# Local attention by halves of head pairs, with row factors in the exponential and rotary rows gathered by DMA

## The chip, the cores and the metric

The kernel runs on one core of a Trainium2 chip. The metric is device time in microseconds for one execution. Each core has TensorE (PE, matrix products, whose weight loads are shown apart as PEld), VectorE (DVE), ScalarE (ACT), GpSimd (POOL) and a queue engine (SP) that here issues nearly all DMA transfers. Each engine works through its own instructions in the order in which they were built; an instruction that waits holds up all behind it on its engine.

## The reference

A decoder of two layers, model width 1024, 512 tokens and 16 meta tokens ahead of them. Layer 0 mixes tokens by gated linear attention, layer 1 by sliding-window attention over one shared set of keys and values. Around each mixer stand two feed-forward blocks. Every block has a norm before it and one after. The part that matters here is the mixer of layer 1 (cut):

```python
q = (hn @ w_q)                          # hn = rmsnorm(h): 16 heads of 64, 4 query heads per key head
q = apply_partial_rope(q, cos, sin) * 64 ** -0.5       # the first 16 of 64 columns are rotated
# per block of 128 queries: 16 meta keys, 128 keys of the block before, 128 of its own
s = jnp.einsum('bkgnqd,bknsd->bkgnqs', q_blk, k_band)
mask: meta all visible; previous block j > i and blk > 0; own block j <= i
m = jnp.maximum(jnp.max(s, axis=-1, keepdims=True), sink)
p = jnp.exp(s - m)
p = p / (jnp.sum(p, axis=-1, keepdims=True) + jnp.exp(sink - m))
o = p @ v_band ; mix = o @ w_out
```

The norm's factor is one number for each token (row factor): the projection can use the unnormed rows, and the factor can be applied to q later.

## The kernel before

Activations lie transposed: 128 channels on the partitions, tokens along the row. A float32 operand is split into a high and a low part (`split`, L405; `split_part`, L224), and a product takes three matmuls (`mm3s`, L333). Weights come as 128x512 raw tiles, in eight buffers, by DMAs that SP issues (`load_unit`, L274). ACT copies the high part and DVE subtracts it for the low part.

What sets the order: every stage is written as generator jobs under `Flow` (L60), a clock of estimates that only matmuls advance. A job says by `yield` how long its results will take, and the recorded instructions of a job are put between the matmuls of the main thread. The framework then fixes the order on each engine when it builds the program. PSUM has eight tiles (`pp`, L133).

Layer 1's mixer is `swa` (L1062). `x_first` (L509) does the projection of the first four of eight units for tokens in two groups of 256, while the residual step of the block before (`Residual.run`, L453) still makes the operands of the second group, on DVE and ACT. `x_units` (L486) does units 4 to 7, 512 tokens wide. One unit is a pair of heads, which share the 128 partitions (e = 0 and 1). `evac` (L1079) takes each result out of PSUM with `rope` (L997), four DVE operations over all 128 channels. The row factor of each token, spread over all partitions by a matmul (`rstd`, L348, tile r_l1m) and copied by ACT, is first multiplied into the tables of cosine and sine (tile csq, L1083), so q leaves `rope` with factor, rotation and 1/8 in it.

`soft` (L1095) is the first half of attention for one unit. It makes scores for four blocks and two heads (tile sc), copies them to SBUF (L1118) and masks by copy_predicated (L1119, tile s, or Y for the first units). Then follow the maximum (L1123), the exponential with the sum (L1131, tile den), and the division: the meta part goes to tile mt (L1139), head 0 by DVE (L1144), head 1 by ACT (L1142). `core` (L1146) transposes the probabilities (L1160, tile pt, and ptm for the meta part), copies them (L1165), masks a second copy (L1166) and multiplies by the values (tile o, L1176 to L1181). Own and previous block are one product with the previous block's values and one with the difference (dv). `split` makes so, the operand of `out_proj` (L552), which gives y: units 0 to 3 first, 512 tokens wide, written to Y; then units 4 to 7, 256 wide and added. A unit waits for the second unit before it, and units 4 to 7 for the core of the third before it (`LAG`, L48).

## Time and profile before

| | us |
|---|---|
| median of 3 runs (1934.33 to 1935.24) | 1934.42 |
| the profiled execution | 1935.17 |
| its span | 1933.4 |
| PE busy in the span | 1888.9 |
| first scores of the mixer start at | 1431.7 |
| 256-wide half of its output projection starts at | 1538.1 |

The times of a trace are counted from the start of the span. A row of a window lists start and end, its length, the busy time of PE, PEld, DVE, ACT and POOL with the number of instructions, the granted clock (1.00 is full), the share of the DMA engines and GB/s. A row of a wait names who waited for whom, the total in us, how many times, and the longest. A row of the chain has a start, a length, and what ran then. A group has busy time, mean ns of one, and idle time before it with what ended it. Where two operations follow each other on one engine they overlap by some 0.1 us, so a chain's length by its count is less than the duration of one.

### The profile page before, as it was taken

How to read it: one execution, taken by the hardware profiler on the slowest of the kernel's cores; microseconds unless marked ns; L12 is line 12 of the kernel's file. 1: busy time of each engine (PE TensorE's matmuls, PEld its weight loads, DVE VectorE, ACT ScalarE, POOL GpSimd, SP SyncE). 2: the span in 40 equal slices, each digit the busy share in tenths (PEclk: the TensorE clock that was granted, in tenths of full speed). 3: DMA queues.
4: the chain of work that ended last, by engine and by line, in shares of the span. 5: the costliest groups of instructions: out<-in, count | busy, mean ns of one | idle time of the engine just before them, and what ended most of it. 6: DMA issues, size and time to landing. Idle time of an engine off the chain costs nothing.

```text
span 1933.4 us, 37344 instructions
## 1 busy us (share of the span) xinstructions
PE 1888.9 (98%) x14522; PEld 1802.5 (93%) x14522; DVE 1408.0 (73%) x2853; ACT 1017.9 (53%) x2308; POOL 176.3 (9%) x377
## 2 busy tenths in 40 slices
PE   8999999999999999999999999999998999999997
PEld 8999999999999999999999898989976898989897
DVE  6885858676364788585887786868787679858584
ACT  5663636653245555353574453535647865636363
POOL 2000000321111300000032000000310040000002
PEclk9999999999999999999999999999998999999998
DMA  4332323322113123333351123233321112333331
GB/s 161 107 98 89 105 91 110 110 77 72 39 56 110 56 72 98 100 92 104 98 173 45 61 88 115 89 109 101 130 66 34 63 49 82 96 103 109 102 111 44
DMA packets 102145, 174.55 MB, mean 90 GB/s; under 512 B 11472, under 2 KB 24272, under 8 KB 101968
## 3 DMA queue, kind: packets, MB, share of 16 engines
q1 hardware_dynamic: 101680, 172.05, 28.3%
q8 instruction: 113, 1.85, 0.4%
q14 instruction: 64, 0.52, 0.1%
q10 hardware_dynamic: 288, 0.13, 0.0%
HBM read 170.04 MB, written 2.10 MB: 89 GB/s over the span
## 4 chain that ended last, share of the span: by engine, by line
PE 69%; DVE 19%; ACT 8%; issue 3%; POOL 1%; DMA 0%; SPq 0%; DVEq 0%; ACTq 0%; POOLq 0%
PE y L162 30%; PE x L162 17%; PE a L162 10%; DVE raw L251 5%; DVE w_s L246 4%; PE c L162 3%; ACT w_s L245 3%; DVE w L246 3%; PE d L162 2%; PE o L162 1%; DVE w L227 1%; PE po L162 1%; ACT w L226 1%; DVE hidl1f L775 1%; PE sc L162 1%
## 5 line engine op out<-in xcount | busy, mean ns | idle before, releaser
L246 DVE TENSOR_TENSOR w_s<-raw,w_s 128x512 fp32r<-128x512 f32 x288 | 194.1, 691 | 134.9 <-ACT w_s L245 133.1
L227 DVE TENSOR_TENSOR w<-raw,w 128x512 fp32r<-128x512 f32 x378 | 239.4, 658 | 33.4 <-ACT w L226 31.6
L162 PE MATMUL y<-hidl0f,w 128*128 128x256 f32 (+1 forms) x2112 | 261.1, 285 | 0.0
L162 PEld LDWEIGHTS y<-hidl0f,w 128*128 128x128 f32 x2112 | 258.8, 188 | 0.7
L245 ACT ACTIVATE w_s<-raw 128x512 fp32r<-128x512 f32 x288 | 175.3, 628 | 152.6 <-DVE raw L251 139.3
L162 PE MATMUL y<-hidl1f,w 128*128 128x512 f32 (+1 forms) x1344 | 249.6, 346 | 0.0
L162 PEld LDWEIGHTS y<-hidl1f,w 128*128 128x128 f32 x1344 | 212.3, 188 | 34.1 <-ACT hidl1f L774 0.5
L226 ACT ACTIVATE w<-raw 128x512 fp32r<-128x512 f32 x378 | 209.2, 587 | 49.7 <-PE y L162 42.3
L251 DVE TENSOR_TENSOR raw<-raw,raw 128x512 f32<-128x512 f32 x288 | 198.1, 688 | 5.5
L403 POOL TENSOR_TENSOR acc_post<-acc_post,sq_post 128x256 f32<-128x256 f32 (+1 forms) x72 | 56.9, 791 | 1493.8 <-ACT sq_post L402 1493.0
L246 DVE TENSOR_TENSOR w<-raw,w 128x512 fp32r<-128x512 f32 x216 | 148.3, 688 | 31.1 <-ACT w L245 29.7
L162 PE MATMUL x<-x_l0m,w 128*128 128x272 f32 (+1 forms) x1200 | 158.3, 288 | 0.0
L245 ACT ACTIVATE w<-raw 128x512 fp32r<-128x512 f32 x216 | 133.9, 621 | 41.2 <-PE y L162 40.9
L162 PEld LDWEIGHTS x<-x_l0m,w 128*128 128x128 f32 x1200 | 149.4, 189 | 1.2
L572 DVE TENSOR_TENSOR Y<-y,Y 128x256 f32<-128x256 f32 (+2 forms) x176 | 83.0, 473 | 73.0 <-PE y L162 72.7
L162 PE MATMUL a<-zl0f_t,w_s 128*128 128x264 f32 x864 | 117.8, 285 | 3.8 <-ACT c L751 3.8
L162 PE MATMUL a<-zl1f_t,w_s 128*128 128x256 f32 x864 | 115.0, 282 | 2.0 <-ACT c L751 1.5
L162 PEld LDWEIGHTS a<-zl0f_t,w_s 128*128 128x128 f32 x864 | 110.1, 188 | 5.0 <-ACT c L751 5.0
L162 PEld LDWEIGHTS a<-zl1f_t,w_s 128*128 128x128 f32 x864 | 106.8, 188 | 4.7 <-ACT c L751 4.6
L162 PE MATMUL x<-x_l0f,w 128*128 128x256 f32 (+1 forms) x768 | 101.7, 293 | 6.9 <-ACT w L226 5.9
L162 PEld LDWEIGHTS x<-x_l0f,w 128*128 128x128 f32 x768 | 98.3, 194 | 8.2 <-ACT w L226 6.1
L162 PE MATMUL x<-x_l1f,w 128*128 128x256 f32 (+1 forms) x576 | 93.1, 320 | 0.0
(488 smaller groups left out, 3281.9 us busy)
## 6 DMA issues: line engine op xcount, KB each, us to landing
raw<-in_w_in SPq DMA_DIRECT2D x352, 256.0 KB, 2.9
raw<-in_w_out SPq DMA_DIRECT2D x96, 256.0 KB, 3.4
raw<-in_gla_in SPq DMA_DIRECT2D x50, 256.0 KB, 3.0
raw<-in_w_last SPq DMA_DIRECT2D x48, 256.0 KB, 3.1
raw<-in_w_out SPq DMA_DIRECT2D x64, 128.0 KB, 2.9
raw<-in_gla_out SPq DMA_DIRECT2D x16, 256.0 KB, 2.8
raw<-in_w_q SPq DMA_DIRECT2D x16, 256.0 KB, 3.9
raw<-in_swa_out SPq DMA_DIRECT2D x16, 256.0 KB, 3.0
```

The lines of the kernel that those rows point to most:

```text
L162: inst = pe.matmul(o, lhs, rhs, start=start, stop=stop, skip_group_check=onto)
L226: act.activation(w[:, 0, :m], raw[:, :m], AF.Copy)
L227: dve.tensor_tensor(w[:, 1, :m], raw[:, :m], w[:, 0, :m].bitcast(F32), op=ALU.subtract)
L245: act.activation(w[:, 0, :512], src, AF.Copy)
L246: dve.tensor_tensor(w[:, 1, :512], src, w[:, 0, :512].bitcast(F32), op=ALU.subtract)
L251: dve.tensor_tensor(dst, dst, src, op=ALU.add)
L403: pool.tensor_tensor(sums[0][:, :n], sums[0][:, :n], t[:, :n], op=ALU.add)
L572: dve.tensor_tensor(y, p[:, :n], y, op=ALU.add)
L775: dve.scalar_tensor_tensor(t.hid[:, 1, g], t.h, -1.0, t.hid[:, 0, g].bitcast(F32), op0=ALU.mult, op1=ALU.subtract)
```

## The change

Attention runs in sixteen visits, each for one unit and one half of the tokens (two blocks): the first half of units 0 to 3, their second half, then the same for units 4 to 7. A visit's four score columns, 576 wide, are divided by one DVE multiply, and the meta part is copied afterwards.

The row factors are no longer spread over the partitions. `root` (the first part of the old `rstd`) leaves them as columns, tokens on the partitions (tile roots). They enter as the scale of the exponential, and are multiplied into the maximum. So `evac` is one ACT copy with the factor 1/8 and waits for no factor, and neither does its drain in `x_first` and `x_units`.

The rotary rows, 16 of each head's 64, are gathered by eight DMAs of SP from the q tiles of four units into one tile of 128 partitions (`turn`), turned by four DVE operations, and put back by eight DMAs. There is a turn for each of the two token groups of units 0 to 3, and one for units 4 to 7. The tables in memory are laid out for it (cosp, sinp). The meta values need 64 partitions instead of 128. The second call of `out_proj` waits for the second halves of units 4 to 7 only ahead of its second token group. The diff, cut (in the body of `swa` mainly the added lines are shown; the lines that they replace stand in the listing above):

```diff
--- before.py
+++ after.py
@@ -45,7 +45,9 @@
 STAGGER = 5.0
 SOFT = 5.0
 NORM = 3.0
-LAG = 3
+LAG = 4
+TURN = 3.5
+PROBS = 1.4
 NEG = -1e30
 
 V_GAIN = 0
@@ -345,7 +347,7 @@
         mm3s([(o, w)], j, x, g, start, stop)
 
 
-    def rstd(sq, n, dim, half, name, eng=pool):
+    def root(sq, n, dim, name, eng, yv=None):
         c = 128 if n % 128 == 0 else n // 4
         nch = n // c
         st = ps(f"st_{name}")
...
@@ -379,6 +382,11 @@
             pool.tensor_tensor(zz, zz, aa, op=ALU.mult)
             pool.tensor_scalar(zz, zz, -0.5, 1.5, op0=ALU.mult, op1=ALU.add)
             pool.tensor_tensor(yy, yy, zz, op=ALU.mult)
+        return yy
+
+    def rstd(sq, n, dim, half, name, eng=pool):
+        yy = root(sq, n, dim, name, eng)
+        c, nch = yy.shape
         dg = sm.tile([P, 272], F32, tag="dg", name=f"dg_{name}", bufs=2)
         eng.tensor_tensor(
             dg[:c, :n].rearrange("p (j c) -> p j c", c=c),
...
@@ -434,6 +444,12 @@
             square_into(self.accs[gi], H[:, k, o : o + n], k, KD, f"{self.name}_{o}_{k}")
 
         def factors(self, gi, eng=pool):
+            if self.column is not None:
+                o, n = self.groups[gi]
+                yield FACT
+                root(self.accs[gi], n, D, f"{self.name}_{o}", eng, self.column[:, 2 * gi : 2 * gi + 2])
+                yield CHAIN
+                return
             if self.rt is None:
                 self.rt = sm.tile([P, TOK], F32, tag="R", name=f"R_{self.name}", bufs=2)
             o, n = self.groups[gi]
...
@@ -549,7 +569,7 @@
 
 
 
-    def out_proj(hid, groups, split_groups, first, finish=None, tailm=0, packed=False):
+    def out_proj(hid, groups, split_groups, first, finish=None, tailm=0, packed=False, second=()):
         nh = len(hid)
         ws = []
 
@@ -593,6 +613,8 @@
         if not finish:
             return
         for gi, g in enumerate(split_groups):
+            if gi:
+                flow.wait(*second)
             for m in range(KD - tailm, KD):
                 unit(m, g)
                 sq(m, gi)
...
-                transpose(p[:, :P], vm[:, :P])
+                transpose(p[:64, :P], vm[:, :64])
                 for e in range(2):
                     dve.tensor_tensor(
-                        vmz[j][:, 4 * e : 4 * e + 4],
-                        p[:, 64 * e : 64 * e + 64].unsqueeze(1).to_broadcast([P, 4, 64]),
-                        rowm[:, 4 * e : 4 * e + 4].unsqueeze(2).to_broadcast([P, 4, 64]),
+                        vmz[j][:64, 2 * e : 2 * e + 2],
+                        p[:64, 64 * e : 64 * e + 64].unsqueeze(1).to_broadcast([64, 2, 64]),
+                        rowm[:64, 2 * e : 2 * e + 2].unsqueeze(2).to_broadcast([64, 2, 64]),
                         op=ALU.mult,
                     )
                 yield 1.0
@@ -1072,135 +1094,155 @@
             nsink = ap.tile([P, 16], F32, name="nsink")
             dve.tensor_scalar(nsink, vec[:, V_SINK : V_SINK + 16], -1.0, None, op0=ALU.mult)
             cr, sr = duo("csq")
...
+            sp.dma_start(cr, a["cosp"])
+            sp.dma_start(sr, a["sinp"])
+            qd = [None] * 4
 
             def evac(u, g, p):
                 o, n = g
...
+                if qd[u // 2] is None:
+                    qd[u // 2] = pair_tile(f"q{u}", F32)
+                act.activation(qd[u // 2][:, u % 2, o : o + n], p[:, :n], AF.Copy, scale=0.125)
+
+
+            def turn(half, g, after):
                 for jb in after:
                     yield jb
...
+                o, n = g
+                pk, sh = (t[:, o : o + n] for t in duo(f"turn{half}_{o}"))
+                ends = []
+                for d in range(2):
+                    for e in range(2):
+                        at = 64 * d + 32 * e
+                        for c in range(2):
+                            rows = qd[2 * half + d][64 * e : 64 * e + 16, c, o : o + n]
+                            ends.append((rows, pk[at + 16 * c : at + 16 * c + 16]))
+                for rows, packed in ends:
+                    sp.dma_start(packed, rows)
+                yield TURN
+                dve.stream_shuffle(sh, pk, TURN_SHUFFLE)
+                dve.tensor_tensor(pk, pk, cr[:, o : o + n], op=ALU.mult)
+                dve.tensor_tensor(sh, sh, sr[:, o : o + n], op=ALU.mult)
+                dve.tensor_tensor(pk, pk, sh, op=ALU.add)
+                for rows, packed in ends:
+                    sp.dma_start(rows, packed)
+                yield TURN
+
+
+            visits = [(u, hf) for us in (range(4), range(4, KD)) for hf in range(2) for u in us]
+
+            def score_tile(i):
+                u, hf = visits[i]
+                t = flat(Y)[:, (i - 4) * 576 : (i - 3) * 576] if i // 4 == 1 else flat(pair_tile(f"s{u}_{hf}", F32))[:, :576]
+                return t.rearrange("p (c t) -> p c t", t=144)
+
+            def soft(i, after):
+                for jb in after:
+                    yield jb
+                u, hf = visits[i]
+                if i == 1:
                     yield STAGGER
                 j = u // 4
...
+                qq = qd[u // 2][:, u % 2]
+                s = score_tile(i)
+                nm, den, es = (sm.tile([P, 4], F32, tag=t, name=f"{t}{u}_{hf}") for t in ("nm", "den", "es"))
+                probs[i] = s
 
                 keys = kz[j].rearrange("p b c -> p (b c)")
...
+                for c in range(2):
+                    b = 2 * hf + c
                     k0, n = (META + 144 * (b - 1), 272) if b else (0, 144)
                     pst = []
                     for e in range(2):
                         rows = slice(64 * e, 64 * e + 64)
                         pst.append(ps(f"sc{u}_{e}{b}"))
                         mm(pst[e][:, :n], qq[rows, META + b * P : META + (b + 1) * P], keys[rows, k0 : k0 + n])
...
+                    for e, p in enumerate(pst):
+                        act.activation(s[:, 2 * e + c], p[:, n - 144 : n], AF.Copy)
+                        dve.copy_predicated(s[:, 2 * e + c, META:], mgt, p[:, :P] if b else neg)
+                    yield SCORE
+                while x.rjob[hf] is None:
+                    yield SCORE
+                yield x.rjob[hf]
+                rc = x.column[:, 2 * hf : 2 * hf + 2]
+                pairs = lambda t: t.rearrange("p (e c) -> p e c", c=2)
+                sinks = lambda t: t[:, 2 * u : 2 * u + 2].unsqueeze(2).to_broadcast([P, 2, 2])
+                dve.tensor_reduce(nm, s, axis=AX.X, op=ALU.max, negate=True)
+                dve.tensor_tensor(pairs(nm), pairs(nm), rc.unsqueeze(1).to_broadcast([P, 2, 2]), op=ALU.mult)
+                dve.tensor_tensor(pairs(nm), pairs(nm), sinks(nsink), op=ALU.min)
+                dve.tensor_tensor(pairs(es), pairs(nm), sinks(vec[:, V_SINK : V_SINK + 16]), op=ALU.add)
+                for c in range(4):
+                    act.activation(
+                        s[:, c], s[:, c], AF.Exp, scale=rc[:, c % 2 : c % 2 + 1], bias=nm[:, c : c + 1],
+                        accum_out=den[:, c : c + 1],
+                    )
                 act.activation(es, es, AF.Exp)
                 yield SOFT
                 dve.tensor_tensor(den, den, es, op=ALU.add)
                 dve.reciprocal(den, den)
...
+                dve.tensor_tensor(s, s, den.unsqueeze(2).to_broadcast([P, 4, 144]), op=ALU.mult)
+
+            def core(i):
+                yield softs[i]
                 yield NORM
+                u, hf = visits[i]
                 j = u // 4
...
+                s = probs[i]
+                mt = sm.tile([P, 64], F32, tag="mt", name=f"mt{u}_{hf}")
+                dve.tensor_copy(mt.rearrange("p (c m) -> p c m", m=META), s[:, :, :META])
+                pm = ps(f"ptm{u}_{hf}")
+                transpose(pm[:64, :P], mt)
+                ptm = sm.tile([64, P], F32, tag="ptm", name=f"pm{u}_{hf}", bufs=2)
+                act.activation(ptm, pm[:64, :P], AF.Copy)
+                p = ps(f"pt{u}_{hf}")
+                for c in range(4):
+                    transpose(p[:, c * P : (c + 1) * P], s[:, c, META:])
+
+                pt = pair_tile(f"pt{u}_{hf}", F32)
+                pta, ptc = (pt[:, i, :512].rearrange("p (c k) -> p c k", k=P) for i in range(2))
+                pb = p.rearrange("p (c k) -> p c k", k=P)
+                act.activation(pta, pb, AF.Copy)
+                own = (lambda t: t) if hf else (lambda t: t[:, 1::2])
+                dve.tensor_tensor(own(ptc), own(pb), mle.unsqueeze(1).to_broadcast([P, 4 if hf else 2, P]), op=ALU.mult)
+                yield PROBS
+                o = ps(f"o{u}_{hf}")
 
                 kvh = [slice((2 * j + e) * 64, (2 * j + e) * 64 + 64) for e in range(2)]
...
+                for c in range(2):
+                    b = 2 * hf + c
+                    oo = [o[64 * e : 64 * e + 64, c * P : (c + 1) * P] for e in range(2)]
                     for e in range(2):
...
+                        mm(oo[e], vt[:, max(b - 1, 0), kvh[e]], pta[:, 2 * e + c], True, False)
                     for e in range(2):
                         if b:
...
+                            mm(oo[e], dv[:, b - 1, kvh[e]], ptc[:, 2 * e + c], False, False)
                     for e in range(2):
...
+                        mm(oo[e], vmz[j][:64, 2 * e + c], ptm, False, True)
+                if so[u] is None:
+                    so[u] = pair_tile(f"so{u}")
+                split(so[u], o[:, :256], (META + 256 * hf, 256))
 
             so = [None] * KD
...
+            probs, softs, cores = [None] * 16, [], []
+
+            def attend(i, *after):
+                softs.append(flow.spawn(soft(i, [*after, *softs[max(i - 2, 0) : max(i - 1, 0)]])))
+                cores.append(flow.spawn(core(i)))
 
             drained = x_first(x, 4, evac, first_ahead=5)
...
+            turns = [flow.spawn(turn(0, g, [drained[gi]])) for gi, g in enumerate(L1)]
+            for i in range(8):
+                attend(i, turns[i // 4], *cores[max(i - LAG, 0) : max(i - LAG + 1, 0)])
+            x_units(x, 4, L1W, lambda i, g, p: evac(4 + i, g, p))
+            turned = flow.spawn(turn(1, L1W[0], []))
+            for i in range(8, 16):
+                attend(i, turned, cores[i - LAG])
+            flow.wait(*cores[:8])
             out_proj(so[:4], L1W, L1, True, packed=True)
...
+            flow.wait(*cores[8:12])
             set_ahead(16)
             cap[0] = used[0] + 8
...
+            out_proj(so[4:], L1W, L1, False, finish, KD, True, cores[12:])
 
 
     dve.memset(ones, 1.0)
@@ -1280,6 +1322,7 @@
         kv, placed = shared_kv(nxt, kp, [again(0), again(1)])
         x.rt, x.rjob = nxt.rt, nxt.rjob
         nxt, fin = into("l1m", 1, 1, True, lambda k: gain(1, 2, k), L1)
+        nxt.column = kp.tile([P, 4], F32, name="roots")
         ffn(x, L1W, fin)
         x = nxt
         nxt, fin = into("l1f1", 1, 3, False, lambda k: gain(1, 4, k), L1)
@@ -1295,6 +1338,7 @@
     0.0014142135623842478, 0.00027424818836152554, 5.3182957344688475e-05, 1.0313385246263351e-05,
 ]
 ROT_SHUFFLE = list(range(8, 16)) + list(range(8)) + list(range(16, 32))
+TURN_SHUFFLE = [i ^ 8 for i in range(32)]
 
 
 def _tiles(w, kt, mt):
@@ -1350,6 +1394,7 @@
         ct[r : r + 8], ct[r + 8 : r + 16] = cos, cos
         st[r : r + 8], st[r + 8 : r + 16] = -sin, sin
     c["cos"], c["sin"] = ct, st
+    c["cosp"], c["sinp"] = np.tile(np.concatenate([cos, cos]), (8, 1)), np.tile(np.concatenate([-sin, sin]), (8, 1))
     return {n: np.ascontiguousarray(v) for n, v in c.items()}
 
 
```

107 lines of the change are left out of this document (11 added, 96 removed).

## The prediction

> **What bounds the kernel now.** I read the busy totals, then the windows, the waits and the chain of waits around the attention of layer 1. First the totals, the windows (busy time of PE, PEld, DVE, ACT, POOL with counts, granted clock, DMA share, GB/s), and the waits between 1380 and 1580:
>
> ```profile
> PE 1888.9 (98%) x14522; PEld 1802.5 (93%) x14522; DVE 1408.0 (73%) x2853; ACT 1017.9 (53%) x2308; POOL 176.3 (9%) x377
> ...
> 1410.00:1432.00 22.00, 19.38 (x136) 17.24 (x136) 15.37 (x46) 6.71 (x16) 6.56 (x17) 1.00 0.07 25
> ...
> 1450.00:1462.00 12.00, 5.86 (x36) 3.70 (x34) 10.04 (x32) 11.99 (x52) 0.00 (x0) 0.96 0.01 3
> 1462.00:1487.00 25.00, 22.54 (x189) 18.87 (x191) 14.28 (x39) 16.40 (x63) 0.00 (x0) 0.81 0.14 42
> 1487.00:1508.00 21.00, 19.85 (x135) 14.39 (x134) 15.12 (x49) 17.31 (x74) 0.00 (x0) 1.00 0.08 26
> 1508.00:1538.00 30.00, 30.00 (x286) 24.87 (x284) 17.79 (x46) 23.07 (x77) 0.00 (x0) 1.00 0.14 44
> ...
> DVE den L1134 <- ACT es L1132: 16.5, 8, 3.3
> ...
> PE o L162 <- ACT pt L1165: 5.4, 3, 2.5
> ...
> PE ptm L174 <- DVE mt L1139: 2.5, 1, 2.5
> ...
> PE r_l1m L162 <- POOL dg_l1m L383: 2.0, 1, 2.0
> ```
>
> TensorE bounds the program, and the stage that the change rewrites is where it is idle: 2.6 us in 1410 to 1432, then 6.1, 2.5 and 1.2, 12.4 in all. It waits for probabilities (pt, mt), which wait for the exponentials. From 1508 to 1538 it is never idle: there the matmuls of the output projection fill every gap. Now pieces of the chain, and PE's timeline (start, length):
>
> ```profile
> 1440.11 2.04 PE x L162 x8
> ...
> 1461.91 4.96 PE o L162 x42
> ...
> 1481.69 4.28 PE o L162 x42
> ...
> 1528.15 3.67 PE y L162 x15
> ...
> 1535.57 2.55 PE o L162 x44
> 1538.12 14.09 PE y L162 x117
> ...
> 1409.61 0.63 PE L162 MATMUL x<-zeros 128*128 128x512 f32 x2
> ...
> 1431.72 0.97 PE L162 MATMUL sc<-kz,q 64*128 64x144 f32 x8
> ...
> 1486.59 1.91 PE L162 MATMUL sc<-kz,q 64*128 64x144 f32 x16
> ```
>
> After its idle spells PE ran at half rate: 42 products in 4.96 and 4.28 us where 44 take 2.55, so 2.5 and 1.8 us more. The most that a better order could win is thus about 12.4 + 4.3 = 16.7 us. The marks for the sum: second token group starts at 1409.6, first scores at 1431.7, scores of units 4 and 5 at 1486.6, and the 256-wide second half of the output projection at 1538.1. Rates: 14.09/117 = 0.12 us a 256-wide matmul, 2.04/8 = 0.255 and 3.67/15 = 0.245 a 512-wide one.
>
> **Totals barely move.** What one DVE or ACT operation takes when others follow (chain), dependent small ones (DVE timeline), and groups by line:
>
> ```profile
> 1489.88 1.41 DVE s L1119 x7
> ...
> 1493.34 1.19 DVE w L227 x2
> 1494.53 1.32 DVE nm L1123 x2
> ...
> 1496.62 3.30 ACT s L1131 x16
> ...
> 1500.05 0.17 DVE L1134 TENSOR_TENSOR den<-den,es 128x8 f32<-128x8 f32 x1 [1.72 <-ACT es L1132]
> 1500.25 0.20 DVE L1135 RECIPROCAL den<-den 128x8 f32<-128x8 f32 x1
> 1500.49 0.23 DVE L1139 TENSOR_TENSOR mt<-s,den 128x64 f32<-128x64 f32 x1
> ...
> L1144 DVE TENSOR_TENSOR s<-s,den 128x512 f32<-128x512 f32 x4 | 2.7, 684 | 0.0
> ...
> L1001 DVE TENSOR_TENSOR q<-x,csq 128x256 f32<-128x256 f32 x8 | 3.3, 410 | 0.0
> ...
> L1001 DVE TENSOR_TENSOR q<-x,csq 128x512 f32<-128x512 f32 x4 | 2.7, 675 | 0.0
> ...
> L1131 ACT ACTIVATE s<-s,nm 128x144 f32<-128x144 f32 x36 | 14.4, 403 | 2.5 <-DVE nm L1126 2.5
> ...
> L1142 ACT ACTIVATE s<-s,den 128x128 f32<-128x128 f32 x20 | 6.3, 394 | 0.0
> ...
> L1155 ACT ACTIVATE pt<-ptm 128x128 f32<-128x128 f32 x8 | 2.2, 277 | 0.9 <-PE ptm L174 0.9
> ```
>
> - PE: the two row-factor matmuls of the mixer go; eight small transposes of meta probabilities come; scores, transposes and products keep their number. Nothing within 1 us.
> - Rotary on DVE: twelve calls of four operations become three. 36 operations go at about 0.34 to 0.6 (rows less 0.08 overlap), two thirds of them 256 wide: some 17 us. The two scalings of the tables go too.
> - DVE per visit (one unit, one half), by the spacings above: four masked copies 0.8, reduction 0.66, three small ones on the maximum 0.55, denominator 0.45, one 576-wide multiply 0.67, meta copy 0.13, mask 0.34 or 0.6, split of the output 0.34: about 4.05. Sixteen are 65 us; a unit now, with the same prices, is 6.1, eight are 49. So +16: it cancels what rotary gives.
> - ACT: 32 scalings of probabilities go (0.3 each, 10 us); q copies come (8 of 256, 4 of 512, some 4 us); 64 exponentials get a second per-partition operand, the row factor. A copy of 128 with such an operand took 0.394 (the scaling), without 0.277, so the operand costs about 0.1; whether a second costs as much beside the bias no row shows. Bounds 0 and 64 x 0.117 = 7.5 us. I take 0.1 each, as the scaling is the same kind of operand: a visit's four exponentials 1.65 (3.30/2) become 2.05.
>
> The Trainium skill speaks here against the change (ScalarE: Activation LUTs, What ACT_TABLE_LOAD costs): each per-partition pointer operand adds about 93 ns; 64 of them would be 6 us by an estimate from that page, and with none the sum below would end 4 us lower. The first operand agrees with it by 117 ns; no run yet shows a second.
>
> **The sum, along the built order of the instructions, from mark to mark.**
>
> (1) Front. DVE no longer does rotary between the residual's steps, and ACT no longer stands waiting for the row factors, so the second group's operands come in time; no matmul waits for the factors. From 1409.6: zeros 0.6, 96 x 0.12 = 11.5, sums of squares about 0.8, first late unit 24 x 0.255 = 6.1: 1428.6. Before, that point was 1431.7. Gain 3. But the first scores now stand 15 matmuls later (3.8): 1432.4.
>
> (2) First turn. Rows for a small transfer, an issue and a slow transfer:
>
> ```profile
> out<-H SPq DMA_DIRECT2D x16, 128.0 KB, 1.8
> ...
> rowm<-in_rowmask SPq DMA_DIRECT2D x1, 4.0 KB, 2.4
> ...
> L1075 SPq DMA_DIRECT2D csq<-in_cos x1: 328/328/328, 1386.8 to 1386.8; - x1
> ...
> H<-in_h SPq DMA_DIRECT2D x4, 272.0 KB, 5.4
> ```
>
> A turn is 8 issues (2.6 us), a landing, four DVE operations, 8 issues and a landing. No row shows a transfer inside the chip's own memory; I take 2.4 as the size is nearest, bounds 1.8 to 5.4. On SP most of the return of group 1 stands behind the gathers of group 2, whose q is copied at about 1423, so the third return is issued near 1426 and lands near 1428.5: hidden, with 4 us to spare; at 5.4 it would cost a little. Weight loads wait behind these on SP, but their splits are needed tens of us later: nothing.
>
> (3) Visits 0 to 6, up to the second turn. This turn serves units 4 to 7 at once; its q is complete when the last projection ends near 1453 and its gathers land by 1459. But its DVE operations stand in DVE's order behind visits 0 to 6. From about 1435.5: seven visits less the unfinished ends 28, seven weight splits at 0.6 (1.19/2) 4, uncovered waits for exponentials about 5 (now 2.05 us, covered where two visits interleave): 1472.5. Then shuffle, two multiplies and an addition with two weight splits between them, six at 0.6: 1476; third return 1.0 + 2.4: scores of unit 4 near 1479.5. On PE these scores stand right behind the transposes of visit 5 (unit 1, second half), done by 1470. So PE waits some 9 us here with visits 5 and 6 queued behind, and nothing fills it: all projections of q are already done, and the output projection needs them. The clock after it: two spells cost 4.3 before; here I take 2, plus 1 for the broken stretch before it: 1482.5, against 1486.6 now. Lead 4.
>
> (4) Units 4 to 7. PE's remaining work is the same in both, and before it took 1538.1 - 1486.6 = 51.5 with no idle time. After: PE starts with three old outputs to finish and two pairs of visits in flight. A pair takes DVE 8.1 plus about 1.8 of exponentials that nothing covers, 9.9; four pairs 39.6, lead-in about 10: last product at 1532. By then only 45 of the 96 512-wide projection matmuls have been used as filler; the other 51 stand behind it: 51 x 0.245 = 12.5. The mark of 1538.1 moves to 1544.5. That is +6.4. From there on nothing differs (the second tokens of units 4 to 7 are needed 11 us later and are ready).
>
> The smaller products for meta values in the shared keys stage shorten four DVE operations under a continuous matmul stream: nothing; without that cover, 1 us of gain. The profiled execution took 1935.2 (span 1933.4), 0.04% over the median 1934.4; against the median the forecast is 1934.4 + 6.4, rounded 1941.
>
> **Rivals.**
>
> - Faster: the finer grain closes PE's gap at unit 4. A half visit needs half the exponentials before PE can go on, and the 16.5 us that DVE waits are for those. If they no longer hold DVE, it comes to the second turn by 1462, and the scores of unit 4 start as soon as PE is there, near 1471; neither the 9 us wait nor its 3 us of clock occur. With (4) at the same 62 us the mark is at 1533 and the time 1929. It decides at 1538.1 - 62 = 1476 for unit 4's scores; faster by 0.2% needs 1472. Against it: DVE's total doesn't fall, and a half visit still waits for 2 us of exponentials. 0.24.
> - No change: the lead of (1) and (3) pays the tail of (4) exactly, operand free (4 less) and clock kept (2 less): 1935. 0.16.
> - Much slower: the return of the turn takes the 5.4 us of the slow row, and the scores of both halves wait: 3 more in (3), 2 in (2), and two more spells at half clock (2.5 each): 1951. 0.12, within the slower side.
> - The clock. By the half rate seen after two spells of idle time, a 9 us wait is followed by some us at half speed. If it lasts while DVE sets the pace, it is hidden: 2 less, 1939; if it lasts through (4)'s first pair, 3 more, 1944. The Trainium skill (TensorE: Matmul & The Clock Gate, What's actually happening) has the clock halved after an idle window of about 3.4 us and whole after a busy one, which by an estimate from that page makes at most 1.7 us of loss after the wait; the window of 1462 to 1487 with 0.81 agrees that a drop is short.
>
> **How the numbers follow.** About 0.2% (3.9 us) is what a measurement of this kernel can tell from no change. Forecast with its own spread 1938.5 to 1948: 0.48; much slower 0.12; no change 0.16; faster 0.24. Hence slower 0.60. The range goes from 1926, the faster case with 3 of the 4 us of a free operand, to 1954, past the much slower one. The slower side's own range is 1938.5 to 1954.
>
> **What would show it.** Right: r_l1m gone from PE and the first late unit ended near 1428; PE idle for 7 us or more before unit 4's scores, released by a DMA; the exponentials' group at about 495 ns; DVE without a fall in total; some 50 matmuls 512 wide in one run behind the last product. Wrong: unit 4's scores before 1476; exponentials still at 403; PE above 95% in (4) with the mark before 1538; or the first scores late because of the first turn.

## The result, and the profile after

The changed kernel takes 1953.99 us (median of 4 runs, 1952.96 to 1956.39), the kernel before in the same comparison 1934.49: a ratio of 1.0102 (95% interval 1.0084 to 1.0119). The forecast was 1941 us. The direction was right, but only 6.6 of the 19.5 us were foreseen. The profiled execution, the slowest of the four, took 1956.39 us (span 1954.6).

Totals from the page, and the windows with the columns of the prediction:

```profile
PE 1908.0 (98%) x14526; PEld 1806.3 (92%) x14526; DVE 1404.3 (72%) x2868; ACT 1024.3 (52%) x2310; POOL 173.8 (9%) x375
```
```profile
1450.00:1462.00 12.00, 10.90 (x83) 6.74 (x81) 8.86 (x32) 9.58 (x37) 0.00 (x0) 1.00 0.23 65
1462.00:1487.00 25.00, 15.82 (x102) 9.67 (x101) 16.80 (x54) 15.89 (x63) 0.00 (x0) 0.73 0.10 27
1487.00:1508.00 21.00, 20.31 (x111) 12.20 (x111) 9.49 (x35) 10.47 (x42) 0.00 (x0) 0.50 0.04 10
1508.00:1538.00 30.00, 27.88 (x220) 17.49 (x219) 20.30 (x74) 21.62 (x82) 0.00 (x0) 0.95 0.00 1
```

TensorE's busy time rose by 19 us (1888.9 before) for four instructions more, and DVE's total hardly moved. From 1487 to 1508 PE counts as 97% busy, but the granted clock is 0.50 all through. Now the waits between 1380 and 1580, and PE's timeline:

```profile
DVE den L1181 <- ACT es L1179: 21.7, 16, 3.4
...
PE sc L164 <- DMA q<-turn: 6.4, 1, 6.4
...
PE ptm L176 <- DVE mt L1192: 5.2, 4, 1.4
```
```profile
1411.21 0.63 PE L164 MATMUL x<-zeros 128*128 128x512 f32 x2
...
1432.94 0.52 PE L164 MATMUL sc<-kz,q 64*128 64x144 f32 x4
...
1486.69 1.60 PE L164 MATMUL sc<-kz,q 64*128 64x144 f32 x4 [6.38 <-DMA q<-turn]
...
1547.78 25.91 PE L164 MATMUL y<-so,w 128*128 128x512 f32 x168
```

The second token group starts 1.6 us later than in the trace of before (1409.6), ahead of nearly all that was changed. This is scatter between executions: over the kernels here it lies between 1407.7 and 1411.2, and e4_before64 below, in which nothing ahead of that point differs from the kernel before, has 1411.1. The last run holds 168 entries; the 256-wide part of it is the 117 of before, so 51 are 512 wide, and the mark of 1538.1 stands at about 1547.8 + 51 x 0.245 = 1560.3.

DMAs and groups (the SP row: shortest/median/longest issue in ns, then the stretch in which they were issued):

```profile
turn<-q SPq DMA_DIRECT2D x16, 16.0 KB, 1.8
...
q<-turn SPq DMA_DIRECT2D x8, 32.0 KB, 2.2
```
```profile
L1121 SPq DMA_DIRECT2D turn<-q x24: 507/580/1294, 1411.6 to 1461.1; - x24
```
```profile
L1175 ACT ACTIVATE s<-s,nm,roots 128x144 f32<-128x144 f32 x48 | 23.7, 496 | 3.7 <-DVE nm L1172 2.4 <-DVE nm L1171 1.2
```

### The profile page after: what moved, and what is told of

Read it like the earlier page. It is cut to its first block, busy times and chain, and to the rows that moved or that the text cites. A ratio compares the mean times of both kernels' runs of the same rounds, so it can differ in the third digit from the quotient of the medians.

```text
span 1954.6 us, 37474 instructions
## 1 busy us (share of the span) xinstructions
PE 1908.0 (98%) x14526; PEld 1806.3 (92%) x14526; DVE 1404.3 (72%) x2868; ACT 1024.3 (52%) x2310; POOL 173.8 (9%) x375
## 4 chain that ended last, share of the span: by engine, by line
PE 69%; DVE 19%; ACT 7%; issue 3%; POOL 1%; DMA 1%; SPq 0%; DVEq 0%; ACTq 0%; POOLq 0%
PE y L164 30%; PE x L164 16%; PE a L164 10%; DVE raw L253 5%; DVE w_s L248 4%; PE c L164 3%; ACT w_s L247 3%; DVE w L248 3%; PE d L164 2%; PE o L164 1%; DVE w L229 1%; PE po L164 1%; ACT w L228 1%; PE sc L164 1%; DVE hidl1f L797 1%
```

## The experiments

The framework orders the instructions anew for each kernel, so an edit can also move neighbours; where it moved none, the text says so. Times are medians, in brackets the ratio to the kernel before with its 95% interval. The kernel before had a median of 1934.7 to 1935.8 us in these comparisons.

### 64-row meta products

What had been missed was seen in the timeline. In the kernel before, four entries of the products by the values take 0.22 us each time, whatever follows:

```profile
1474.06 0.39 PE L162 MATMUL o<-pt,vt 128*64 128x128 f32 x4
1474.28 0.39 PE L162 MATMUL o<-pt,dv 128*64 128x128 f32 x4
1474.50 0.39 PE L162 MATMUL o<-pt,vmz 128*64 128x128 f32 x4
1474.72 0.39 PE L162 MATMUL o<-pt,vt 128*64 128x128 f32 x4
```

In the changed kernel, at full clock too, the meta products (vmz) have 64 rows:

```profile
1534.94 0.44 PE L164 MATMUL o<-pt,vt 128*64 128x128 f32 x4
1535.21 0.39 PE L164 MATMUL o<-pt,dv 128*64 128x128 f32 x4
1535.53 0.44 PE L164 MATMUL o<-pm,vmz 64*64 64x128 f32 x4
1535.90 0.44 PE L164 MATMUL o<-pt,vt 128*64 128x128 f32 x4
```

From vt to vt it is 0.96 us where it was 0.66. There are two such stretches in each of 16 visits. Half the rows cost more time, not less. Three kernels test it. Three theories of the loss were in the field: K, these products; W, the wait for the turn of units 4 to 7 and the half rate behind it; S, the order by halves itself.

**e1_meta128**, the meta products over 128 rows again:

```diff
-                mt = sm.tile([P, 64], ...)
-                dve.tensor_copy(mt..., s[:, :, :META])
+                mt = sm.tile([P, P], ...)
+                dve.tensor_copy(mt..., s[:, :, :META].unsqueeze(1).to_broadcast([P, 2, 4, META]))
-                        mm(oo[e], vmz[j][:64, 2 * e + c], ptm, False, True)
+                        mm(oo[e], vmz[j][:, 2 * e + c], ptm, False, True)
```

> The changed kernel with its meta products over 128 rows again (the meta probabilities stand twice, the second copy meets zero rows of the meta values). In the changed kernel's trace a block's 12 entries (vt, dv, meta) take 0.95 us at full clock where they took 0.65 before, and each return from 64 rows to 128 seems to cost 0.3 us: 32 such runs are 10 us of TensorE. Theory K (the 64-row products are the missed cost, and keep the clock at half too): 12 entries take 0.65 us again, the half rate ends within some 10 us, the time falls by 10 to 20 us to 1934 to 1944. Theory W (the wait for the turn of units 4 to 7 halves the clock and keeps it there): the products get shorter, but the 6.4 us wait and about 40 us at half rate stay; time 1945 to 1952. Theory S (the order by halves is simply slower, bound by DVE and ACT): 1950 or more.

**e5_grouped**, the two 64-row groups of a visit next to each other, in an order that is otherwise that of the changed kernel:

```diff
+                    if c:
+                        for e in range(2):
+                            mm(oo[e], vmz[j][:64, 2 * e + c], ptm, True, False)
...
-                    for e in range(2):
-                        mm(oo[e], vmz[j][:64, 2 * e + c], ptm, False, True)
+                    if not c:
+                        for e in range(2):
+                            mm(oo[e], vmz[j][:64, 2 * e + c], ptm, False, True)
```

> The changed kernel with the order of a visit's products changed: the meta products of its two blocks stand next to each other (first block's last, second block's first), so TensorE goes from 128 rows to 64 and back once in a visit and not twice, 16 changes there and back in place of 32. Theory K: each costs 0.3 us at full and 0.4 us at half rate, so 5 to 6 us of TensorE time go, and 3 to 6 us of the time: 1948 to 1951. Theories W and S: within 1.5 us of 1954.

**e4_before64**, the kernel before with the same handicap; the order on every engine is exactly that of before:

```diff
-                        mm(oo[e], vmz[j][:, 4 * e + b], ptm, False, True)
+                        mm(oo[e], vmz[j][64 * e : 64 * e + 64, 4 * e + b], ptm[64 * e : 64 * e + 64], False, True)
```

> The kernel before with its meta products over 64 rows: each head takes the 64 rows of the meta probabilities and values that are its own (the other 64 are zeros), nothing else changes. Theory K (each run of 64-row products and back costs 0.3 us of TensorE): 32 runs, 10 us of TensorE; in before's schedule about half stand where TensorE is the pace, and some half-rate time is added: 1939 to 1943. If the loss comes only with the order by halves: within 2 us of 1935.4.

Measured: e1_meta128 1949.10 (1.0069, 1.0054 to 1.0084), e5_grouped 1950.48 (1.0081, 1.0066 to 1.0096), e4_before64 1944.73 (1.0052, 1.0037 to 1.0067). With 128 rows the groups of four entries of e1_meta128 stand 0.22 apart again:

```profile
1536.39 0.39 PE L164 MATMUL o<-pt,dv 128*64 128x128 f32 x4
1536.61 0.39 PE L164 MATMUL o<-pm,vmz 128*64 128x128 f32 x4
1536.83 0.39 PE L164 MATMUL o<-pt,vt 128*64 128x128 f32 x4
```

In e5_grouped eight 64-row entries in one run cost about 0.3 us once. That is read from the trace; the 3.5 us that e5_grouped is shorter in all are not clear of noise, since its interval overlaps that of the changed kernel:

```profile
1529.92 0.39 PE L164 MATMUL o<-pt,dv 128*64 128x128 f32 x4
1530.23 0.65 PE L164 MATMUL o<-pm,vmz 64*64 64x128 f32 x8
1530.82 0.44 PE L164 MATMUL o<-pt,vt 128*64 128x128 f32 x4
```

In e4_before64 the run behind the last product starts 9.6 us after the 1538.1 of before, with the same 117 entries:

```profile
1411.07 0.63 PE L162 MATMUL x<-zeros 128*128 128x512 f32 x2
...
1547.75 14.11 PE L162 MATMUL y<-so,w 128*128 128x256 f32 x117
```

Of the 9.6 us, 1.5 stand at the start of the second token group already (1411.1 against 1409.6), ahead of the edit. The other 8.2 are 32 such places by 0.26 us, and by the medians e4_before64 is 10.0 us longer, more than expected (1939 to 1943), so in this order nearly all of the cost is on the path. It is the cleanest of all these runs. In the changed kernel the places cost about 5 us on the path (1954.0 to 1949.1), while TensorE's busy time falls by 16.6 (1908.0 to 1891.4, in part because less of it is at half rate): the rest lay where TensorE waits for others. K is right for this part, but had expected 10 us or more of e1_meta128, whose time lies in the range of W; the other 15 us are elsewhere. The Trainium skill (TensorEngine Tiling (Array Packing), Key Properties) says that a change of the tiling mode, and not only of the tile, drains TensorE. The trace agrees, and puts a number to it: 0.3 us there and back; whether it is a drain that takes this time, no run here can tell. In e1_meta128 the wait for the turn is 8.2 us and the longest stretch at half clock is from about 1478 to 1491.

### The turns, and the wide products

**e2_rope_dve**, the rotation on DVE at the eviction, no turns; **e12_both**, the same with the edit of e1_meta128:

```diff
-                act.activation(qd[u // 2][:, u % 2, o : o + n], p[:, :n], AF.Copy, scale=0.125)
+                rope(qd[u // 2][:, u % 2, o : o + n], p[:, :n], cr[:, o : o + n], sr[:, o : o + n], ...)
-            turned = flow.spawn(turn(1, L1W[0], []))
-                attend(i, turned, cores[i - LAG])
+                attend(i, cores[i - LAG])
```

> The changed kernel with the rotation on DVE at each eviction as in the kernel before (tables times 1/8, no row factor), without the DMAs and turns; halves, columns and 64-row products stay. Theory W: the 6.4 us wait ahead of unit 4's scores goes and with it most of the half rate, 10 us or more come back: 1936 to 1944. Theory K: half rate stays over 30 us since the products stay as they are; the gain is the wait less the DVE work that comes back (16 evictions of 4 operations): 1948 to 1957. Theory S: no gain, 1953 to 1960, DVE being longer by some 10 us.

> The changed kernel with both undone that e1_meta128 (meta products over 128 rows, 5 us less) and e2_rope_dve (rotation on DVE, no turns, 12 us less) undid alone; visits by halves and row factors as columns stay. If these two are all of the loss and independent, 17 us come back: 1935 to 1939, beside 1935.4 for the kernel before. If the visits themselves (shorter instructions, twice the waits) or the scale column of the exponential cost something of their own, or if both remedies buy the same half-rate time, 1940 to 1944.

**e7_hybrid**, 128 rows, the turns kept for units 0 to 3 alone:

```diff
+                if u < 4:
                     act.activation(d, p[:, :n], AF.Copy, scale=0.125)
+                else:
+                    rope(d, p[:, :n], c2[:, o : o + n], s2[:, o : o + n], ...)
```

> The changed kernel with meta products over 128 rows, the turns by DMA for units 0 to 3 alone, and the rotation on DVE at the eviction for units 4 to 7. In e2_rope_dve DVE was full from 1430 to 1450 and TensorE had 6 us of gaps there, in the changed kernel's trace the same place has next to none. If the turns of the first four units are a gain and only the turn of units 4 to 7 is a loss: 3 to 6 us less than e12_both, 1931 to 1936. If the four DVE operations for each of units 4 to 7 (11 us in all) delay the visits as much as the turn did: 1938 to 1945.

Measured: e2_rope_dve 1942.09 (1.0033, 1.0020 to 1.0047), e12_both 1938.46 (1.0022, 1.0012 to 1.0032), e7_hybrid 1944.51 (1.0052, 1.0037 to 1.0067). So, against the rotation on DVE, all turns together cost 11.9 us with 64 rows and 10.6 with 128, and of the latter units 0 to 3 cost 6.1 and units 4 to 7 4.6 (this last step is at the edge of the noise: the intervals of e7_hybrid and e1_meta128 overlap). e2_rope_dve lies where W had it, and its windows bear on the clock: it has all the 64-row products, but no turn to wait for, and its clock is whole from 1462 to 1538, where the changed kernel has 0.73, 0.50 and 0.95. The windows from 1432 to 1538, e2_rope_dve and then the changed kernel:

```profile
1432.00:1538.00 106.00, 95.92 (x661) 60.62 (x660) 81.10 (x259) 75.92 (x273) 0.00 (x0) 0.97 0.16 51
```
```profile
1432.00:1538.00 106.00, 91.50 (x589) 57.02 (x588) 68.96 (x233) 68.82 (x255) 0.00 (x0) 0.82 0.16 47
```

So the 64-row products alone do not hold the clock at half. Whether the wait does it, or the lack of wide products around it, is not separated here, and how much of the 11.9 us is half rate stays open.

That e7_hybrid would beat e12_both, the first of its two expectations, was wrong: the part that looked free was the dearer one. The windows of tile x alone (the projection; PE's busy time and count first) show why. e12_both, then e7_hybrid:

```profile
1425.00:1445.00 20.00, 11.89 (x50) 8.46 (x50) 4.40 (x15) 0.91 0.33 103
1445.00:1465.00 20.00, 6.57 (x19) 3.69 (x19) 1.41 (x3) 0.83 0.18 57
1465.00:1490.00 25.00, 8.00 (x30) 5.21 (x29) 2.71 (x6) 0.92 0.07 22
```
```profile
1425.00:1445.00 20.00, 17.11 (x68) 12.10 (x67) 3.34 (x8) 0.00 (x0) 1.00 0.51 156
1445.00:1465.00 20.00, 2.26 (x10) 1.50 (x8) 0.68 (x1) 0.00 (x0) 0.83 0.12 43
1465.00:1490.00 25.00, 0.00 (x0) 0.00 (x0) 1.42 (x3) 0.00 (x0) 0.86 0.07 22
```

An eviction that is quick and waits for nothing lets the wide products of units 4 to 7 run early. They are then missing in the visits' gaps up to 1490, and 45 wide products of the output projection are left behind the last visit where e12_both has 15 (162 and 132 entries less 117). **e14_hold** puts them back by order alone; **e18_hold7**, with (0, 0, 0, 2), and **e19_hold67**, with (0, 0, 1, 4), vary how much is held:

```diff
         for i in range(nu):
+            if hold:
+                hold(i)
             w = next_w()
...
-            x_units(x, 4, L1W, lambda i, g, p: evac(4 + i, g, p))
+            x_units(x, 4, L1W, lambda i, g, p: evac(4 + i, g, p), lambda i: flow.wait(*cores[: (0, 0, 2, 4)[i]]))
```

> e7_hybrid with one thing more: the projection of unit 6 is put in order behind the first two visits and that of unit 7 behind the first four. In e7_hybrid and the changed kernel the last wide products of units 4 to 7 end by 1458 and the next (y) start after 1495, in e12_both the evictions hold them back so that they run until 1485. Theory F (the turn of units 0 to 3 costs by letting these fillers run too early, so TensorE has nothing wide between 1458 and 1495 and 30 more y products stay behind the last visit): wide products stand all through, fewer than 120 entries left of the run behind the last visit where e7_hybrid has 162, and 4 to 7 us come back: 1937 to 1941. If the turn of units 0 to 3 costs in another way (its DMAs, DVE): 1943 or more.

> e14_hold, but only the projection of unit 7 is held back, behind the first two visits; unit 6 stays where e7_hybrid has it. In e14_hold TensorE waited 9.5 us ahead of the first transposes, since both units were held; here unit 6 fills part of that stretch. If it is the spread of the wide products that counts: 2 to 5 us under e14_hold, 1934 to 1937. If one held unit is too little for 1458 to 1495: between e14_hold (1939) and e7_hybrid (1944.5).

> e14_hold, with unit 6 held behind the first visit alone and unit 7 behind the first four. If TensorE's wait of 9.5 us ahead of the first transposes is what keeps e14_hold at 1939: 1 to 4 us less, 1935 to 1938. If DVE and ACT set the end there: 1939 again.

Measured: e14_hold 1939.33 (1.0022, 1.0013 to 1.0031), e18_hold7 1947.58 (1.0054, 1.0037 to 1.0071), e19_hold67 1940.38 (1.0027, 1.0018 to 1.0036). In e14_hold the products of the projection stand in 1465 to 1490, and 12 wide ones are left behind the last visit (129 entries, where fewer than 120 were expected):

```profile
1425.00:1445.00 20.00, 7.77 (x32) 5.37 (x30) 2.60 (x6) 0.00 (x0) 0.88 0.48 150
1445.00:1465.00 20.00, 3.17 (x9) 1.53 (x9) 0.00 (x0) 0.00 (x0) 0.77 0.06 23
1465.00:1490.00 25.00, 10.80 (x39) 6.79 (x39) 2.73 (x6) 0.00 (x0) 1.00 0.07 22
```

So 5.2 of the 6.1 us that the turn of units 0 to 3 costs come back by order alone; its DMAs are not what costs. How many to hold isn't settled: with one unit held, 48 stayed behind and nothing was gained, which neither of its expectations had; and the 9.5 us that TensorE waits in e14_hold ahead of the first transposes were not what keeps it at 1939, or e19_hold67 would be faster.

### The scale column of the exponential

**e8_imm** is e7_hybrid, **e16_imm128** is e1_meta128, each without the column; the row factors are left out, and the maximum is multiplied by ones in their place:

```diff
-                        s[:, c], s[:, c], AF.Exp, scale=rc[:, c % 2 : c % 2 + 1], bias=nm[:, c : c + 1],
+                        s[:, c], s[:, c], AF.Exp, bias=nm[:, c : c + 1],
```

> e7_hybrid with the exponential's scale left at one and the maximum times one: the row factors of the tokens are left out, so the output is another; all operations stay in number and place. An exponential goes from some 496 to 403 ns, 64 of them are 6 us of ACT. If ACT paces the visits (den waits for es, 16 times): 2 to 5 us less than e7_hybrid. If TensorE or DVE pace them: within 1 us of it.

> e1_meta128 (both turns, 128 rows, visits by halves) with the exponential's scale left at one and the maximum times one: the row factors are left out, so the output is another; all operations stay in number and place. If the column costs here what it cost in the order of e7_hybrid: 6 to 8 us less, 1941 to 1943. If it costs as much as the prediction's sum had for it: 4 less, 1945. If it is hidden, since the turn of units 4 to 7 holds the visits anyway: 1948 or more.

**e9_before_col** gives the kernel before a column of ones:

```diff
-  act.activation(s[:, b], s[:, b], AF.Exp, bias=nm[:, e, b : b + 1], ...)
+  act.activation(s[:, b], s[:, b], AF.Exp, scale=ones[:, 0:1], bias=nm[:, e, b : b + 1], ...)
```

> The kernel before with a column of ones as scale of its 64 exponentials, nothing else. Each takes 93 ns more, 6 us of ACT in all. If ACT paces the visits in before's schedule as in e7_hybrid and e8_imm: 1938 to 1942. If the cost belongs to the order by halves: within 1.5 us of 1934.7.

Measured: e8_imm 1937.08 (1.0016, 1.0006 to 1.0025), 7.4 us under e7_hybrid; e16_imm128 1942.33 (1.0038, 1.0024 to 1.0052), 6.8 under e1_meta128; e9_before_col 1944.74 (1.0052, 1.0038 to 1.0066), 9.7 over the kernel before. Group, wait and last run of e9_before_col:

```profile
L1131 ACT ACTIVATE s<-s,nm,ones 128x144 f32<-128x144 f32 x36 | 17.7, 496 | 2.3 <-DVE nm L1126 2.3
```
```profile
DVE den L1134 <- ACT es L1132: 24.2, 8, 4.1
```
```profile
1548.04 14.17 PE L162 MATMUL y<-so,w 128*128 128x256 f32 x117
```

An exponential took 403 ns in the kernel before and takes 496 here. 64 x 93 ns are 6.0 us of ACT, and DVE's wait for the exponentials rose from 16.5 to 24.2 us, 7.7: DVE waits for all of it. More than 6 us appear on the path, and more than had been expected of e8_imm (2 to 5 us) and of e9_before_col (1938 to 1942). The rest may have a second cause that these runs mix in: in these three kernels the shorter or longer exponential also moved some instructions' order by a few places. The e9 run's own clock was at half for longer, too (0.70 in 1450 to 1462, 0.96 in the kernel before); between e1_meta128 and e16_imm128 it is not (0.89 in 1432 to 1538 in both), and the difference is still 6.8.

### The halves alone

**e13_halves** is e12_both with the row factors back in the tables:

```diff
+                if u == 0:
+                    for t in (cr, sr):
+                        dve.scalar_tensor_tensor(t[:, o : o + n], t[:, o : o + n], 0.125, x.rt[:, o : o + n], ...)
-                        s[:, c], s[:, c], AF.Exp, scale=rc[:, c % 2 : c % 2 + 1], bias=nm[:, c : c + 1],
+                        s[:, c], s[:, c], AF.Exp, bias=nm[:, c : c + 1],
```

> Visits by halves alone: e12_both with the row factors back in the tables of cosine and sine as in the kernel before (the eviction waits for them again), so the exponential has no scale column and the maximum no extra multiply. e8_imm was 7.4 us under e7_hybrid by the scale column alone. If the visits by halves cost nothing of their own, the time falls under e12_both by 4 to 7 us: 1931 to 1935, level with the kernel before or a little faster. If the halves cost (twice as many waits, shorter instructions): 1937 or more.

Measured: 1935.30 us, ratio 1.0002 (0.9993 to 1.0011). Visits by halves, with the smaller parts of the edit that stay in this kernel (the one multiply by DVE for a visit, the later wait in the second `out_proj`), neither win nor lose: theory S falls, and so does the hope that the finer grain closes gaps. Steps from there to the changed kernel: columns 3.2 us (e12_both; the price of the exponentials less what it gains that no eviction waits for a factor), 64 rows 3.6 (e2_rope_dve, whose interval overlaps that of e12_both), turns 11.9, which makes the 18.7 from 1935.3 to 1954.0. In another order the parts share differently (64 rows 4.9 when they are put in last); they are not independent.

### The clock

**e3_warm** and **e17_warm128** put twelve unused products ahead of unit 4's scores, in the changed kernel and in e1_meta128; **e15_warm** puts fourteen ahead of the first transposes of e13_halves. In the first two the order on every engine stays as it was, but for the added products; in e15_warm neighbours moved as well:

```diff
+                if i == 8:
+                    warm = ps("warm").rearrange("p (a c) -> p a c", c=P)
+                    for _ in range(12):
+                        pe.matmul(warm, zeros, zeros.unsqueeze(1).to_broadcast([P, 4, P]), start=True, stop=True)
```

> The changed kernel with twelve 512-wide products of zeros, unused, put on TensorE ahead of unit 4's first scores, where it waits 6.4 us for the turn (12 take 5.9 us at half rate, so they fit in the wait). Theory W (the clock stays at half because TensorE idles or works thinly there): the clock is whole when unit 4's scores start, the products of 1487 to 1511 run at full rate, 8 to 15 us less: 1939 to 1946. Theory K with the clock held down by the 64-row products: the clock rises for a moment and falls again, under 4 us gained: 1950 to 1955. If the half rate costs nothing (DVE and ACT set the pace): the clock is whole and the time stays within 2 us of 1954.

> e1_meta128 with the twelve unused 512-wide products of zeros of e3_warm ahead of unit 4's first scores. In e1_meta128 the clock is at half from 1478 to 1491, behind the waits. If the clock there is on the path: 3 to 7 us less, 1942 to 1946. If DVE and ACT set the pace of units 4 to 7 once the products are over 128 rows: within 1.5 us of 1949.

> e13_halves with fourteen unused 512-wide products of zeros where TensorE waits 3.5 us ahead of the first transposes (1445.7 to 1449.3), into the tile that the transposes overwrite. In e13_halves the clock is at half from 1449 to 1456 behind that wait. If the half rate follows from the idle stretch and is on the path: full clock there, 2 to 3 us less, 1932 to 1933.5. If DVE and ACT pace the visits there: within 1 us of 1935.3.

Measured: e3_warm 1951.36 (1.0089, 1.0069 to 1.0109), of four runs two at 1946.9 and 1948.1 with a mean clock of 0.993, two at 1954.7 and 1955.0 with 0.987; e17_warm128 1948.55 (1.0070, 1.0055 to 1.0085); e15_warm 1936.66 (1.0010, 1.0001 to 1.0019). Windows of e13_halves and then e15_warm:

```profile
1445.00:1450.00 5.00, 1.47 (x8) 1.00 (x7) 5.00 (x18) 2.04 (x10) 0.00 (x0) 0.90 0.43 125
1450.00:1455.00 5.00, 3.99 (x28) 2.98 (x27) 3.33 (x11) 2.90 (x14) 0.00 (x0) 0.50 0.24 84
```
```profile
1445.00:1450.00 5.00, 4.31 (x25) 3.26 (x25) 4.17 (x14) 1.14 (x4) 0.00 (x0) 1.00 0.53 157
1450.00:1455.00 5.00, 5.00 (x35) 3.01 (x35) 2.56 (x12) 3.79 (x20) 0.00 (x0) 1.00 0.14 53
```

In e15_warm the clock stays whole where it was at half, and the time is no better. That doesn't show that the half rate was free there, since the order moved too; and among its own eleven executions the two with a mean clock of 0.997 took 1935.2 and 1935.5 us, the two with 0.994 1937.5 and 1937.9. e17_warm128 gained nothing (0.6 us), but it is no test: its clock was at half for as long as that of e1_meta128, only elsewhere (0.78, 0.78 and 0.94 in the three windows from 1462 to 1538, against 0.74, 0.91 and 0.89). From 1432 to 1538, e1_meta128, e17_warm128 and e3_warm:

```profile
1432.00:1538.00 106.00, 83.57 (x643) 61.19 (x643) 71.47 (x241) 73.55 (x272) 0.00 (x0) 0.89 0.16 47
```
```profile
1432.00:1538.00 106.00, 87.92 (x624) 64.42 (x624) 71.74 (x242) 72.38 (x269) 0.00 (x0) 0.89 0.16 47
```
```profile
1432.00:1538.00 106.00, 92.92 (x660) 59.96 (x660) 72.03 (x243) 74.93 (x274) 0.00 (x0) 0.92 0.16 49
```

In e3_warm the runs with the higher clock are some 7 us shorter, but its interval overlaps that of the changed kernel, so a gain by the edit isn't shown. That a higher clock and a shorter time go together holds in the changed kernel and in all sixteen of the experiments: within a kernel, 0.001 more of mean clock, which is about 3.9 us less at half rate, goes with about 1.2 us less time (a line through the 107 executions on record, each kernel about its own mean). Which of the two causes the other isn't shown by that. How much of the 19.5 us the half rate costs in the changed kernel stays open.

## Why the prediction was right or wrong

(1) **Front: right.** First scores were forecast 22.8 us after the start of the second token group (1409.6 to 1432.4), and came 21.7 after it (1411.2 to 1432.9).

(2) **First turn: right as far as it went.** Landing took 1.8 us (2.4 taken), the issue 0.58 where 0.33 was taken; the first scores did not wait. What the turn does by letting wide products run early stood in (4), as the 51 left behind.

(3) **Up to the second turn: right in kind, some 6 us short.** DVE was to reach this turn at 1472.5 and unit 4's scores to come near 1479.5; the mark of 1482.5 has the 3 us for the clock on top. In the trace DVE is there at 1480.3, and the scores come at 1486.7; 1.6 us of either is the later start. DVE's waits between 1435 and the turn, and the turn itself:

```profile
DVE den L1181 <- ACT es L1179: 10.1, 7, 3.4
```
```profile
1480.30 0.72 DVE L1123 STREAM_SHUFFLE turn<-turn 128x512 f32<-128x512 f32 x1
```

The sum had "uncovered waits for exponentials about 5"; they were 10.1, and DVE waited another 3.7 us for other things, which the sum had at nothing. The return of the turn released the scores, as forecast. PE waited 6.4 us and not 9, since the visits ahead of it on PE were slower too: their last transposes ended at 1480.3 and not by 1470.

(4) **Units 4 to 7: here it failed.** The 51 products left behind came out to the number, and so did their price. But the last product came 61.1 us after unit 4's scores (1486.7 to 1547.8), where 49.5 were forecast from the mark (1482.5 to 1532), or 52.5 from the scores at 1479.5 with the clock's 3 us in them. Three terms:

- "Scores, transposes and products keep their number. Nothing within 1 us" is the step that failed first. The number was kept, the shape not. I had looked at the smaller meta values only where they are made, and put them at nothing. They cost 5 us here, and 8 to 10 in the kernel before. The trace of before has no such products by the values to price them by, but their place between 128-row ones could be read in the built order. e1_meta128 takes 55.2 us for the stretch (1483.7 to 1538.9).
- The scale column was seen and priced right by the instruction (0.1 us taken; 496 - 403 = 93 ns measured). Of its effect on the end the sum had 4 us; 6.8 were measured (e16_imm128). I had taken part of it as covered between interleaved visits; the runs show no such cover. The Trainium skill (ScalarE: Activation LUTs, What ACT_TABLE_LOAD costs) has about 93 ns for a pointer operand, and the trace agrees: 93 ns. e16_imm128, without the column and with 128 rows, takes 52.0 us for the stretch (1482.9 to 1534.9), about the 52.5 of the sum, which had the column in it.
- The clock was put at 3 us in all. The windows shown add up to some 37 us at half rate (25 x 0.27 x 2, 21, and 30 x 0.05 x 2), where 25 us at 0.81 made 10 before. The estimate of at most 1.7 us of loss after the wait, from the Trainium skill (TensorE: Matmul & The Clock Gate, What's actually happening), doesn't hold here: the window of 1487 to 1508 has PE 97% busy and stays at 0.50. The prediction saw its estimate confirmed by the window of 1462 to 1487 of the kernel before; but 0.81 over 25 us is some 9.5 us at half rate (25 x 0.19 x 2), and no short drop. How much of the half rate lies on the path is open.

Of the 13 us between forecast and result, the 64 rows are 5 and the column 3. Without both (e16_imm128) the time is 1942.3, and the sum less its 4 us gives 1937: 5 us are left. Some 4 us stand ahead of the turn, in (3): even in e16_imm128 DVE reaches it 67.0 us after the start of the second token group (1410.1 to 1477.1), where the sum had 62.9 with the column in it, and DVE still waits 7.5 us for exponentials on the way. Unit 4's scores at 1482.9 look as forecast there only because the mark of 1482.5 has the clock's 3 us in it. What lengthens these waits, the clock or the order of the visits, isn't settled.

**The rivals.** "Faster" needed unit 4's scores before 1476 and a grain that closes gaps: e13_halves shows that the grain alone gives nothing. "Much slower" named a slow return of the turn: the landing of 2.2 us refutes its mechanism, though its 1951 was the nearest number. That the result lies inside the range, at its very end (1954), is luck: the range reached so far for that rival's sake. The variant of the clock that "lasts through (4)'s first pair" is what the trace shows; at 1944 it was too small.

**The signs named ahead.** r_l1m is gone from PE, the group of exponentials is at 496 ns, DVE's total is level, 51 wide products stand in one run: as said. PE's wait was 6.4 and not 7 or more.

## What to carry to other kernels

When an edit changes a matmul's row count, price it by where it stands among its neighbours: here a few 64-row products between 128-row ones cost 0.3 us for each excursion, and full rows with zeros in them were faster. An operand that costs 0.1 us on an engine that is half idle was paid in full here, where it lies in the chain from score to probability. And an eviction that gets quicker may spend the wide products early that were filling the gaps of a later stage; count what is left behind the last step.

## What the runs showed of the hardware that was not expected

- Products over 64 rows put between products over 128 rows take longer than with 128 rows: 0.96 us against 0.66 for twelve entries, and one run of eight costs 0.3 us where two runs of four cost 0.6.
- The clock can stay at half for 21 us in a row while PE shows 97% busy, its work there being scores, transposes and small products; in e3_warm it was whole during twelve 512-wide products of zeros, and in e15_warm it was whole, behind such products, through a stretch that had 0.50 without them. In e2_rope_dve, with the same small products but no wait for a turn, it was whole from 1462 to 1538.
- SP took 0.5 to 0.6 us to issue a transfer of 16 or 32 KB inside the chip, where a table's load from memory took 0.33 to 0.42; the landing took 1.8 to 2.2 us, no longer than loads.
